# Swapping two DMA queues in the attention stage: key, query and value loads to SyncE, gates, branch weights and memory outputs to GpSimd

## The chip, the cores and the metric

One Trainium2 chip, of which the program uses one core. The metric is the device time of one execution in microseconds (us). The profile is one execution of the same program, taken by the hardware profiler. SP is the engine that does nothing here but issue DMAs; GpSimd (POOL) issues DMAs too, but also runs elementwise work.

## What is computed

A decoder block over 1024 positions of width 1024: half a feed-forward step, a mixer, half a feed-forward step. The mixer is what matters here:

```
y_a = dsa_attention(...) @ w_dsa_o      # 8 heads, width 64, causal, top-256 keys
y_b = conv_module(...) @ w_conv_out
y_m = memory_attention(...) @ w_mem_o   # 4 heads, into 256 memory tokens
g_a, g_b, g_m = split(sigmoid(gate_logits), 3)
merged = g_a * y_a + g_b * y_b + g_m * y_m
return x + rms_norm(merged @ w_out, mix_post_g)
```

Everything is float32. A product is done as three matmuls on a high and a low part of each operand.

## The kernel before

Earlier stages write what attention needs to DRAM: `qk_spill` (`self.qk`, 8 x 2 x 128 x 1024: four rows of queries, four of keys, each two heads wide, with the high part and the low part as an axis of two), `v_spill`, `gate_spill` (`self.sig`, three gates of 8 blocks of 128 x 1024) and `branch_spill` (`self.br`, the memory attention's outputs). On chip, tiles are taken from 50 slots of 4 KB per partition, alone or in small rings, and a load into a tile can start only when the last reader of that slot is done.

`attn` walks over two halves of the positions (c = 0, 1) and over 8 heads in each. For a head it loads a K tile and a Q tile from the ring `qk` (4 slots, so two heads at a time): `load_stack` (L794) fetches K, and the first half of Q, with the view `self.qk[row, :, e*64:e*64+64, lo:hi]`, whose outermost axis is that axis of two; L822 fetches the second half of Q in two pieces of 64 rows. K is 256 KB in the first half of the stage and 512 KB in the second; Q is 256 KB and twice 128 KB. `load_v` (L787) fetches the value tiles, 512 KB each, for four heads at a time. L851 is the score product, L855 to L861 the softmax, L893 the transposes, L881 the product with V.

`mix` interleaves with this the generator `outputs`, the branch stream: `branch` for the convolution, then for the memory attention (its inputs `om` come at L1110), then for the first half of the attention. Each takes four weight tiles of 512 KB (`weight`, L134), and for each of 8 blocks a gate (`sigr`, L925, ring `st` of two slots), multiplies a product in PSUM by the gate on VectorE (L936) and adds it to the partial sum on GpSimd (L943, in the last branch L938). After `attn` comes the second half of the attention's branch, then the output projection, with weights `woutr`.

A scheduler fixes each engine's order when the kernel is built. TensorE runs its list in that order: if the scores of a head wait for their K or Q, the branch stream's matmuls behind them wait too.

The source of the K load is this:

```
self.nc.gpsimd.dma_start(dst.bitcast(F32), self.qk[row, :, e * 64:e * 64 + 64, lo:hi])
```

Of the kernel before, what the change touches and what calls it, by code (L numbers as in the profile page):

```python
# [8 lines left out]
F32 = mybir.dt.float32  # L9
# [9 lines left out]
P = 128  # L19
# [25 lines left out]
class Kern:  # L45
# [83 lines left out]
        self.nc.scalar.activation(hi, raw, AF.Copy)  # L129
        self.nc.vector.tensor_sub(lo, raw, hi.bitcast(F32))  # L130

    def weight(self, name, src, shape, ring="w", raw="wr"):
        raw = self.rt(raw, name + "r", shape)
        self.nc.sync.dma_start(raw, src)  # L134
        if ring:
            hi, lo = self.rt(ring, name + "h", shape, F32R), self.rt(ring, name + "l", shape, F32R)
        else:
            hi, lo = self.blk(name + "h", shape, F32R), self.blk(name + "l", shape, F32R)
        self.split(hi, lo, raw)
        return hi, lo  # L140
# [640 lines left out]
    def load_v(self, grp, c):  # L781

        nc = self.nc
        V = []
        for t2 in range(2 * c + 2):
            v = self.blk("v", [P, 8, P], F32R)
            nc.gpsimd.dma_start(v.bitcast(F32).rearrange("p (t h) d -> p t (h d)", t=2),  # L787
                              self.vs[2 * t2:2 * t2 + 2, :, grp * 512:grp * 512 + 512].rearrange("t p c -> p t c"))
            V.append(v)
        return V  # L790

    def load_stack(self, dst, row, e, lo, hi):

        self.nc.gpsimd.dma_start(dst.bitcast(F32), self.qk[row, :, e * 64:e * 64 + 64, lo:hi])  # L794

    def behind(self, ins, *before):

# [5 lines left out]
    def attn(self):  # L803


        nc, S = self.nc, self.S
        O = S["O"]
        prev = V = None
        self.filled = None
        for c in range(2):  # L810
            if c:
                self.banks(s=[(0, 1)], tp=[2, 3, 4], po=[5], fl=[6, 7])
            for h in range(H_A):
                e = h % 2
                if e == 0:
                    O.append(self.blk("O", [P, 2, 512], F32R))
                K = self.rt("qk", "K", [P, (4 * c + 4) * P], F32R)
                Q = self.rt("qk", "Q", [P, 2, 512], F32R)
                self.load_stack(K, 4 + h // 2, e, 0, (4 * c + 4) * P)
                self.load_stack(Q[:, 0], h // 2, e, c * 512, c * 512 + 512)  # L820
                for r in range(2):
                    nc.gpsimd.dma_start(Q[r * 64:r * 64 + 64, 1].bitcast(F32),  # L822
                                      self.qk[h // 2, 1 - r, e * 64:e * 64 + 64, c * 512:c * 512 + 512])
                for g in range(2):
                    i0 = 4 * c + 2 * g
                    p, qk = self.weights_of(Q, K, i0)
                    yield (0.2 * i0 + 0.3) * FILL_A[i0 // 4]
                    if prev:
                        yield from self.weigh(*prev, qk)
                    if h % 4 == 0 and g == 0:  # L830
                        if V:
                            self.free(V)
                        V = self.load_v(h // 4, c)
                    prev = (h, g, i0, p, V, O[-1])
        yield from self.weigh(*prev, None)
        self.free(V)
# [78 lines left out]
    def branch(self, get, w, b, halves=(0, 1), last=None, group="fl"):  # L915

        nc, part = self.nc, self.S["part"]
        lo, nh = halves[0] * 512, len(halves) * 512
        first = not part
        for f2 in range(KT // 2):  # L920
            wt = self.weight("wo", w[:, f2 * 256:(f2 + 1) * 256].rearrange("(k p) f -> p k f", p=P), [P, 4, 256])
            for q in range(2):
                f = 2 * f2 + q
                s = self.rt("st", "sigr", [P, nh])
                nc.sync.dma_start(s, self.sig[b, f, :, lo:lo + nh])  # L925
                if first:
                    part.append(self.blk("part", [P, T]))
                for c in halves:
                    py = self.bank(group)
                    cs = slice(c * 512 - lo, c * 512 - lo + 512)  # L930
                    pr = part[f][:, c * 512:c * 512 + 512]
                    for k in range(4):
                        self.filled = self.mm3(py, (wt[0][:, k, q * P:(q + 1) * P], wt[1][:, k, q * P:(q + 1) * P]), get(k, c), k == 0, k == 3)
                        if k == 1:
                            yield 1.3
                    nc.vector.tensor_mul(pr if first else s[:, cs], py, s[:, cs])  # L936
                    if last:
                        nc.gpsimd.tensor_add(s[:, cs], s[:, cs], pr)  # L938
                        mb = self.blk("mg", [P, 2, 512], F32R)
                        self.split(mb[:, 0], mb[:, 1], s[:, cs])  # L940
                        last[c].append(mb)
                    elif not first:
                        nc.gpsimd.tensor_add(pr, s[:, cs], pr)  # L943
                    if c != halves[-1]:
                        yield 1.3
                yield 1.3
# [26 lines left out]
    def build(self):  # L973
        nc, A, S = self.nc, self.A, self.S
# [128 lines left out]
        def outputs():  # L1103
            half = lambda B: lambda k, c: tuple(x[:, c * 512:c * 512 + 512] for x in B[k])
            yield from self.branch(half(cb), A["w_conv_out"], 1)
            self.free(*cb)
            om = [tuple(self.blk("om", [P, T], F32R) for _ in range(2)) for _ in range(4)]
            for h in range(4):
                for r in range(2):
                    nc.sync.dma_start(om[h][r].bitcast(F32), self.br[h, r])  # L1110
            yield from self.branch(half(om), A["w_mem_o"], 2)
            self.free(*om)
            yield from y_a(0, "fl")
            self.free(O[:4])

        fill = outputs()
        self.mix(self.attn(), fill, 1.0)
        for _ in fill:
# [9 lines left out]
        wo = [self.weight("wout", A["w_out"][k * P:(k + 1) * P], [P, D], None) for k in range(KT)]  # L1128
# [7 lines left out]
        for t in range(NT):  # L1136
            c, s = t // 4, slice((t % 4) * P, (t % 4 + 1) * P)
# [348 lines left out]
```

## Time and profile before

| | us |
|---|---|
| time, median of 3 runs (2323.55 to 2325.48) | 2324.51 |
| the profiled execution's own time | 2322.4 |
| its span | 2320.6 |
| TensorE busy in the span | 2229.6 (96%) |
| VectorE busy | 1713.9 (74%) |
| ScalarE busy | 1168.0 (50%) |
| GpSimd busy | 380.9 (16%) |

The attention stage with its branch stream lies at about 1262 to 1524 us of the span, and the second half of the attention's branch at 1524 to 1575. In the page's 40 slices the TensorE digit falls below 9 only at the start, in the 23rd to 25th slice (58 us each, together 1276 to 1450), in the 29th and in the last. The page's DMA section splits the traffic into q1 (hardware, issued by SP: 195.94 MB) and q0 (software, issued by GpSimd: 21.09 MB).

### The profile page before, as it was taken

To read this page: it belongs to the slowest core of one execution; us is meant where nothing else is said; L and a number is where in the kernel's file an instruction comes from. 1 tells how busy PE (TensorE), PEld (TensorE's weight loads), DVE (VectorE), ACT (ScalarE), POOL (GpSimd) and SP (SyncE) were. 2 spreads that over 40 slices of the span, in tenths; PEclk is the share of its full clock that TensorE was granted. 3 is DMA by queue.
4 is the path that set the end of the run, shared out by engine and by line. 5 is a ranking of instruction groups with operands and counts; after the bars stand their busy time and mean duration, and the time that the engine had idled before them with its cause. 6 is when DMAs were issued, how large, how long until landed. Compare 5 with 4: busy or idle time off the path is not lost. (4 is left out here: it accounts for less than half of the span.)

```text
span 2320.6 us, 29086 instructions
## 1 busy us (share of the span) xinstructions
PE 2229.6 (96%) x10800; PEld 1374.5 (59%) x10800; DVE 1713.9 (74%) x3000; ACT 1168.0 (50%) x1971; POOL 380.9 (16%) x338
## 2 busy tenths in 40 slices
PE   8799999999999999999999788999899999999998
PEld 6344444444447987888887677878644444444443
DVE  7887777766577699997558677885877777777657
ACT  6644444444435343598996454453564444444423
POOL 2221111111100000120001213330321111111200
PEclk9799999999999999999999899999999999999999
DMA  8121111111224105334322655443421111111112
GB/s 290 37 64 55 55 60 59 55 55 55 86 70 156 51 28 204 127 123 131 102 96 95 179 153 157 140 155 122 140 78 63 57 60 58 55 55 55 45 56 91
DMA packets 162291, 218.87 MB, mean 94 GB/s; under 512 B 26052, under 2 KB 122820, under 8 KB 162150
## 3 DMA queue, kind: packets, MB, share of 16 engines
q1 hardware_dynamic: 137894, 195.94, 25.8%
q0 software_dynamic: 24256, 21.09, 3.5%
q8 instruction: 84, 1.38, 0.2%
q14 instruction: 57, 0.47, 0.1%
HBM read 171.79 MB, written 45.09 MB: 93 GB/s over the span
## 5 line engine op out<-in xcount | busy, mean ns | idle before, releaser
L146 PE MATMUL banks<-wds,h 128*128 128x512 f16 x704 | 266.8, 379 | 2.5 <-DVE h L262 2.5
L144 PE MATMUL banks<-xh,wts 128*128 128x512 f16 x704 | 267.5, 380 | 0.9 <-ACT xh L282 0.8
L145 PE MATMUL banks<-xl,wts 128*128 128x512 f16 x704 | 267.0, 379 | 0.0
L146 PE MATMUL banks<-xh,wts 128*128 128x512 f16 x704 | 267.0, 379 | 0.0
L145 PE MATMUL banks<-wds,h 128*128 128x512 f16 x704 | 266.8, 379 | 0.0
L144 PE MATMUL banks<-wds,h 128*128 128x512 f16 x704 | 266.7, 379 | 0.0
L1363 DVE SCALAR_TENSOR_TENSOR y<-banks,scal,y 128x512 f32<-128x512 f32 x288 | 209.5, 748 | 76.0 <-PE banks L146 65.6
L144 PE MATMUL banks<-xh,wh 128*128 128x512 f32 x576 | 226.2, 393 | 0.0
L146 PE MATMUL banks<-xh,wl 128*128 128x512 f32 x576 | 226.0, 393 | 0.0
L145 PE MATMUL banks<-xl,wh 128*128 128x512 f32 x576 | 225.4, 391 | 0.0
L144 PE MATMUL banks<-xh,wt 128*128 128x512 f16 x528 | 202.1, 383 | 4.3 <-DVE t L214 2.7
L146 PE MATMUL banks<-xh,wt 128*128 128x512 f16 x528 | 201.6, 382 | 0.8 <-DVE wt L262 0.8
L145 PE MATMUL banks<-xl,wt 128*128 128x512 f16 x528 | 201.6, 382 | 0.0
L261 ACT ACTIVATE wds<-wd,scal 128x1024 f16<-128x1024 f32 x44 | 47.9, 1139 | 252.0 <-DVE scal L230 229.4
L611 DVE SCALAR_TENSOR_TENSOR acc<-u,convc,acc 128x1023 f32<-128x1023 f32 (+14 forms) x120 | 151.7, 1264 | 0.9
L1311 ACT ACTIVATE sil<-sil,scal 128x512 f32<-128x512 f32 x88 | 63.2, 718 | 141.8 <-DVE sil L1310 141.8
L471 ACT ACTIVATE junka<-sc,tk_neg,tk_sg 128x512 bf16<-128x512 f32 (+1 forms) x124 | 124.1, 1001 | 12.4 <-DVE tk_cand L489 9.4
L1216 POOL TENSOR_TENSOR ws<-wg 128x512 f32<-128x512 f32 x22 | 44.8, 2035 | 501.9 <-DVE wds L262 381.1
L245 ACT ACTIVATE junka<-sil 128x1024 bf16<-128x1024 f32 x44 | 46.5, 1057 | 150.9 <-DVE sil L1327 150.9
L146 PEld LDWEIGHTS banks<-xh,wl 128*128 128x128 f32 x576 | 108.4, 188 | 22.4 <-DVE wl L130 0.2
L145 PEld LDWEIGHTS banks<-xl,wh 128*128 128x128 f32 x576 | 108.5, 188 | 21.6
L144 PEld LDWEIGHTS banks<-xh,wh 128*128 128x128 f32 x576 | 108.3, 188 | 21.2 <-ACT xh L129 0.3
(367 smaller groups left out, 4852.6 us busy)
## 6 DMA issues: line engine op xcount, KB each, us to landing
wg<-in_ffn_w_gu SPq DMA_DIRECT2D x44, 512.0 KB, 3.7
wu<-in_ffn_w_gu SPq DMA_DIRECT2D x44, 512.0 KB, 3.6
wd<-in_ffn_w_down SPq DMA_DIRECT2D x44, 512.0 KB, 4.3
wr<-in_w_in SPq DMA_DIRECT2D x38, 512.0 KB, 3.6
gate_spill<-st SPq DMA_DIRECT2D x24, 512.0 KB, 2.8
x_spill<-xres SPq DMA_DIRECT2D x16, 512.0 KB, 2.6
qk_spill<-qst SPq DMA_DIRECT2D x32, 256.0 KB, 2.7
sigr<-gate_spill SPq DMA_DIRECT2D x16, 512.0 KB, 5.0
```

Of the source, the lines that this page charges most:

```text
L144: self.first = mm(out, a[0], b[0], start=start, stop=False)
L145: mm(out, a[0], b[1], start=False, stop=False)
L146: return mm(out, a[1], b[0], start=False, stop=stop)
L245: self.nc.scalar.activation(self.junk(x.shape), x, AF.Square, accum_out=ss)
L261: self.nc.scalar.activation(hi, raw, AF.Copy, scale=s)
L471: nc.scalar.activation(self.junk((P, ns[q])), sc[q], AF.Sign, bias=bias[:, z:z + 1], scale=scale, accum_out=cnt[:, z:z + 1])
L611: nc.vector.scalar_tensor_tensor(a[:, s:], u[:, :T - s], self.cc[:, m, j:j + 1], a[:, s:], op0=OP.mult, op1=OP.add)
L1216: V.tensor_add(a[:, 0], lo[:, :, P:], hi[:, :, P:])
L1311: nc.scalar.activation(o, o, AF.Silu, scale=iv)
L1363: V.scalar_tensor_tensor(self.y[t][:, cs], py, iv, self.y[t][:, cs], op0=OP.mult, op1=OP.add)
```

## The change

Three issue sites, of K, Q and V, go from GpSimd's queue to SP's; the branch stream's weights, gates and memory outputs go from SP's to GpSimd's. `weight` gets an argument for the queue.

```
-    def weight(self, name, src, shape, ring="w", raw="wr"):
+    def weight(self, name, src, shape, ring="w", raw="wr", q=None):
         raw = self.rt(raw, name + "r", shape)
-        self.nc.sync.dma_start(raw, src)
+        (q or self.nc.sync).dma_start(raw, src)
...
-            nc.gpsimd.dma_start(v.bitcast(F32).rearrange("p (t h) d -> p t (h d)", t=2),
+            nc.sync.dma_start(v.bitcast(F32).rearrange("p (t h) d -> p t (h d)", t=2),
...
-        self.nc.gpsimd.dma_start(dst.bitcast(F32), self.qk[row, :, e * 64:e * 64 + 64, lo:hi])
+        self.nc.sync.dma_start(dst.bitcast(F32), self.qk[row, :, e * 64:e * 64 + 64, lo:hi])
...
-                    nc.gpsimd.dma_start(Q[r * 64:r * 64 + 64, 1].bitcast(F32),
+                    nc.sync.dma_start(Q[r * 64:r * 64 + 64, 1].bitcast(F32),
...
-            wt = self.weight("wo", w[:, f2 * 256:(f2 + 1) * 256].rearrange("(k p) f -> p k f", p=P), [P, 4, 256])
+            wt = self.weight("wo", w[:, f2 * 256:(f2 + 1) * 256].rearrange("(k p) f -> p k f", p=P), [P, 4, 256], q=nc.gpsimd)
...
-                nc.sync.dma_start(s, self.sig[b, f, :, lo:lo + nh])
+                nc.gpsimd.dma_start(s, self.sig[b, f, :, lo:lo + nh])
...
-                    nc.sync.dma_start(om[h][r].bitcast(F32), self.br[h, r])
+                    nc.gpsimd.dma_start(om[h][r].bitcast(F32), self.br[h, r])
```

On SP, in the middle of the second half of attention (c = 1), the list before is the branch stream's own; `wor` are branch weights, `sigr` gates:

```order
L134 DMA wor<-in_w_mem_o 128x4x256
L925 DMA sigr<-gate_spill 128x1024 x2
L134 DMA wor<-in_w_dsa_o 128x4x256
L925 DMA sigr<-gate_spill 128x1024 x2
L134 DMA wor<-in_w_dsa_o 128x4x256
```

In the changed kernel the same engine has there:

```order
L794 DMA K<-qk_spill 128x1x1024
L794 DMA Q<-qk_spill 128x1x512
L822 DMA Q<-qk_spill 64x512 x2
L787 DMA v<-v_spill 128x2x512
L794 DMA K<-qk_spill 128x1x1024
L794 DMA Q<-qk_spill 128x1x512
L822 DMA Q<-qk_spill 64x512 x2
L794 DMA K<-qk_spill 128x1x1024
```

From the start of attention to its end nothing but K, Q and V stands on SP, apart from two last gate stores; the output projection's `woutr` loads follow directly behind the last head's.

On GpSimd, at the start of the memory branch's additions (L943), the list before is:

```order
L794 DMA K<-qk_spill 128x1x1024
L794 DMA Q<-qk_spill 128x1x512
L822 DMA Q<-qk_spill 64x512 x2
L943 TENSOR_TENSOR part<-sigr,part 128x512 x3
L794 DMA K<-qk_spill 128x1x1024
L794 DMA Q<-qk_spill 128x1x512
L822 DMA Q<-qk_spill 64x512 x2
L943 TENSOR_TENSOR part<-sigr,part 128x512 x3
```

And in the changed kernel:

```order
L925 DMA sigr<-gate_spill 128x1024
L134 DMA wor<-in_w_mem_o 128x4x256
L943 TENSOR_TENSOR part<-sigr,part 128x512 x2
L925 DMA sigr<-gate_spill 128x1024
L943 TENSOR_TENSOR part<-sigr,part 128x512 x2
L925 DMA sigr<-gate_spill 128x1024
L134 DMA wor<-in_w_dsa_o 128x4x256
L943 TENSOR_TENSOR part<-sigr,part 128x512 x2
```

The additions no longer stand behind K loads, but each pair of them stands between the gate loads whose slots it frees.

In the last branch, where GpSimd's additions (L938) feed the merged tiles, the changed kernel has on GpSimd:

```order
L134 DMA wor<-in_w_dsa_o 128x4x256
L938 TENSOR_TENSOR sigr<-sigr,part 128x512
L134 DMA wor<-in_w_dsa_o 128x4x256
L925 DMA sigr<-gate_spill 128x512
L134 DMA wor<-in_w_dsa_o 128x4x256
L938 TENSOR_TENSOR sigr<-sigr,part 128x512
L134 DMA wor<-in_w_dsa_o 128x4x256
```

Before, the sixteen L938 stand there in one row, with no DMA between them. TensorE's list changes in a few places only, where neighbouring matmuls swap.

## Rows read from the trace of the kernel before

**Rows 1.** Engines by stage (busy us, instructions); then granted clock, DMA share, GB/s.

```profile
core 0: us, PE busy (x) PEld busy (x) DVE busy (x) ACT busy (x) POOL busy (x), PEclk, DMA share, GB/s
1050.00:1100.00 50.00, 50.00 (x223) 41.39 (x222) 35.01 (x81) 43.41 (x78) 2.73 (x4) 1.00 0.42 126
...
1279.00:1361.00 82.00, 63.38 (x344) 51.57 (x342) 56.76 (x170) 39.48 (x99) 22.48 (x33) 0.92 0.65 172
1361.00:1524.00 163.00, 148.67 (x829) 125.92 (x830) 124.43 (x225) 77.09 (x140) 47.19 (x48) 0.96 0.47 139
1524.00:1575.00 51.00, 49.18 (x235) 40.00 (x234) 42.93 (x53) 25.92 (x37) 19.92 (x13) 1.00 0.65 217
```

**Rows 2.** What TensorE waited for, 1240 to 1660: total, times, longest.

```profile
PE banks L851 <- DMA Q<-qk_spill: 21.7, 8, 9.1
PE banks L145 <- DMA om<-branch_spill: 4.8, 2, 3.7
```

**Rows 3.** DMA issues, 1240 to 1600: queue, count, KB each, median us to landing.

```profile
sigr<-gate_spill SPq DMA_DIRECT2D x16, 512.0 KB, 5.0
v<-v_spill POOLq DMA_DIRECT2D x12, 512.0 KB, 8.6
om<-branch_spill SPq DMA_DIRECT2D x8, 512.0 KB, 5.8
K<-qk_spill POOLq DMA_DIRECT2D x8, 512.0 KB, 16.9
wor<-in_w_dsa_o SPq DMA_DIRECT2D x8, 512.0 KB, 4.5
sigr<-gate_spill SPq DMA_DIRECT2D x16, 256.0 KB, 2.9
Q<-qk_spill POOLq DMA_DIRECT2D x14, 256.0 KB, 15.5
```

**Rows 4.** DMA queue q0 (GpSimd's): packets, MB, share; in 1494:1498, then 1436:1440.

```profile
q0 software_dynamic: 75, 0.17, 11.2%
...
q0 software_dynamic: 36, 0.13, 8.2%
```

**Rows 5.** SP's issues of the convolution's constants (first start us), then short stretches, as rows 1.

```profile
L594 SPq DMA_DIRECT2D taps<-in_w_dw x1: 304/304/304, 717.3 to 717.3; - x1
L596 SPq DMA_DIRECT2D taps<-in_conv_ln_b x1: 251/251/251, 718.2 to 718.2; - x1
722.60:722.80 0.20, 0.20 (x2) 0.19 (x1) 0.20 (x2) 0.20 (x1) 0.00 (x0) 1.00 0.07 26
722.80:723.00 0.20, 0.20 (x2) 0.16 (x1) 0.20 (x1) 0.20 (x1) 0.00 (x0) 1.00 0.07 21
1282.00:1286.00 4.00, 4.00 (x26) 3.17 (x25) 2.67 (x10) 1.87 (x7) 0.42 (x1) 1.00 1.10 374
```

**Rows 6.** TensorE in order of time: start, us, tiles [idle before it, and what ended it].

```profile
1298.02 0.45 PE L851 MATMUL banks<-K,Q 128*128 128x128 f32 x1 [9.09 <-DMA Q<-qk_spill]
1364.87 1.69 PE L851 MATMUL banks<-K,Q 128*128 128x320 f32 x4 [5.53 <-DMA Q<-qk_spill]
1508.72 0.75 PE L851 MATMUL banks<-K,Q 128*128 128x320 f32 x4
```

**Rows 7.** GpSimd in order of time, columns as rows 6: the stage's first K load.

```profile
1278.92 0.85 POOL L794 DMA_DIRECT2D K<-qk_spill  x1 [3.12 <-PE banks L851]
```

**Rows 8.** DMA issues in 1266:1269, columns as rows 3.

```profile
v<-v_spill POOLq DMA_DIRECT2D x1, 512.0 KB, 4.7
```

**Rows 9.** What SP's queue waited for, 1240 to 1600: its longest total.

```profile
SPq L925 <- POOL part L943: 97.1, 8, 20.0
```

**Rows 10.** GpSimd's last additions: count, min/median/max ns, first and last start.

```profile
L938 POOL TENSOR_TENSOR sigr<-sigr,part x16: 1274/1294/2204, 1507.2 to 1571.5; 128x512 f32<-128x512 f32 x16
```

**Rows 11.** Stretches of low granted clock, columns as rows 1.

```profile
1292.70:1302.90 10.20, 3.50 (x13) 3.09 (x14) 1.59 (x8) 1.09 (x4) 0.53 (x1) 0.50 0.64 157
...
1364.40:1371.20 6.80, 6.33 (x23) 5.67 (x24) 2.44 (x7) 1.94 (x5) 0.00 (x0) 0.50 0.21 66
```

## The prediction

> **What bounds the kernel now.** I read the stretches first. TensorE is the bound of the whole, and in the attention stage it loses time: 18.6 us idle of 82 in the first part, 14.3 of 163 in the second, 1.8 of 51 behind it [rows 1]. The list of TensorE's waits says where: 21.7 us in eight waits of the scores for Q, loaded on GpSimd's queue, and 4.8 us for the memory outputs [rows 2]. The largest single ones are 9.09 us at 1298 and 5.53 us at 1365 [rows 6]. So the stage is held, now and then, by K and Q landing late. The issue list shows the contrast on which the change plays: K of 512 KB takes 16.9 us from GpSimd's queue, Q of 256 KB 15.5 us, while `om`, gates and weights of 512 KB take 4.5 to 5.8 us from SP's [rows 3]. The question is whether that is the queue or the shape of the load.
>
> **Why K and Q are slow.** V answers half of it: same queue, same 512 KB, but 8.6 us [rows 3], and 4.7 us for one early in the stage [rows 8]. What differs is the view: K and the first half of Q are read through an outermost axis of two, V and `om` through 128 partitions. Late in a head's load, when little else moves, GpSimd's queue had 11.2% of 16 engines' time, which is 1.8 engines, and moved 0.17 MB in those 7.2 engine-us: 23.7 GB/s on each [rows 4]. The other stretch gives 24.8 GB/s. So such a load is confined to about two engines, and the queue has data for them all the time; 374 GB/s is what all sixteen do [rows 5].
>
> Does SP's queue confine too? The convolution's constants are the only narrow loads that SP issues: 31 rows of 2 KB and three single rows, all issued between 717.3 and 718.2. At 722.6 to 723.0 data still moves, at 0.07 of sixteen engines, one engine, and 21 to 26 GB/s [rows 5]. Four loads issued within 1 us, 70 kB in all, and one engine's worth still moving 4 us later: SP's queue confines a narrow load as well, and puts different narrow loads on the same engine. I therefore take it that K and the first half of Q, issued by SP, all go through one pair of engines, head after head.
>
> [...]
>
> **The change, part by part.**
>
> *K, Q, V to SP.* Issuing costs less (0.25 to 0.38 us on SP against 0.85 us on GpSimd [rows 5, 7]), which is off the path. The load itself: on each engine of the pair, a head of the first half needs (262 + 262)/2 kB for K and Q's first half and 262/16 for the two 64-row pieces, 278 kB; a head of the second half (524 + 262)/2 + 16 = 410 kB. Two heads are loaded before the stage; behind the first K load at 1278.9 [rows 7] come six heads of the first kind and eight of the second: 4950 kB. The same two engines carry a sixteenth of all else: 7 V tiles, 14 gates of 512 KB, 6 of 256 KB, 8 weights and 8 `om`, 40 times 512 KB in all (of the loads in rows 3 and the memory branch's four weights, those issued between 1281 and the last head's scores), at 32.8 kB each 1310 kB. Together 6260 kB, at 24.8 GB/s 252 us. The first bytes move some 2 us after the issue (a 256 KB gate takes 2.9 us to land, of which 0.7 is data at 374 GB/s), so the last head's K and Q land at about 1281 + 252 = 1533. Its scores now start at 1508.7 [rows 6]. **+25 us**, if the pair never idles. It hardly can: a head's load is issued when the scores of the head two before are done, and by then the pair is still busy with the head between. At 23.7 GB/s it is 264 us and +36; without the gates', weights' and `om`s' share 209 us, which ends before 1508.7, so the lower end is 0. I take 25, since the share comes through the same engines in any order, and 24.8 is the stretch with the fewest other packets.
>
> The waits of today are not to be subtracted: they are inside 1508.7, and the new ones take their place. TensorE idles ahead of nearly every head from the fourth on, and its static order lets no branch work fill that.
>
> *Branch stream to GpSimd.* 56 loads leave SP. Landing on GpSimd's queue costs 4.7 us at best and 8.6 at the median for 512 KB, against 4.5 to 5.8 now [rows 3, 8]. A gate has two slots and about a block's 10 us until it is used, so 3 us more stays covered. What covers it goes when landing passes some 12 us. The additions L943 come out from behind K loads. SP waited 97.1 us for them [rows 9], but TensorE shows no wait for that, so I cost it at nothing: what is late next is Q anyway.
>
> *The last branch (1524 to 1575).* GpSimd now has an addition of 1.29 us, a gate load (some 0.75 us of issue) and half a weight load per block, about 2.4 us, under the 4.3 us at which the sixteen additions come on average (1507.2 to 1571.5 [rows 10]). TensorE is 49.2 of 51 us busy there [rows 1], so there is little cover: a gate that lands 1 us later through three slots is up to 3 us over eight blocks, a weight load stuck behind a wait some 2 more. Ends 0 and +5; I take **+2**.
>
> *Before the stage.* The first two heads' loads go to SP among the gate stage's weights, at 1047 to 1068. Engine time 4 times 5.3 us on the pair; TensorE never idles there (50.00 of 50 us [rows 1]) and two pairs of weight tiles let a weight come a block ahead: 0. If that cover were gone, up to 5.
>
> *Sum.* 25 + 2 = 27 us on the profiled execution's 2322.4, 2349.4; the median is 2.1 above it: **2351**. The forecast's own range, with the tail's ends, is 2336 (half of the stream's share hidden: 12 us) to 2366 (36 + 5).
>
> **Rivals.**
>
> *1. SP spreads these loads over all engines.* Then K and Q land in about 5 us like `om`, the 21.7 us go, and with them half of TensorE's busy time in the low-clock stretches behind the waits, (3.5 + 6.3)/2, 5 us [rows 11]: about 2298. For it speak the 4.5 to 5.8 us of every wide load on SP; against it the constants' one engine. [...]
>
> *2. Narrow, but not all on one pair.* If K and Q's first half fall on different pairs, the busier engine has 6 x 147 + 8 x 278 + 1310 = 4420 kB, 178 us: not a bound. Landing falls to about 8 and 13 us, the 5.53 us wait and the ones of 1 to 2 us go, the 9.09 us one, behind the V burst, stays: about 2313.
>
> *3. The pair's backlog is just covered.* K, Q and V alone take 209 us of the 228 between 1281 and 1508.7. If the branch stream's packets take no more than the gaps that this leaves, the scores wait about as long as now: 2324, no change. Against it: 40 transfers at 1.3 us are 53 us, and the gaps are 19.
>
> *4. GpSimd's queue becomes a bound too.* The gates land in 15 us instead of 5 (as K does now), two slots turn in 15 + 8 us, 11.5 per block against 10: 1.5 us on 14 blocks, on top of the forecast: 2372.
>
> **How the numbers follow.** Forecast 0.60, rivals in order 0.12, 0.11, 0.08, 0.09. A measurement here can tell about 0.2%, 4.6 us. Faster is rivals 1 and 2: 0.23. Same is rival 3: 0.08. Slower is the forecast and rival 4: 0.69. The range leaves out rival 1 and the upper half of rival 4: 2308 to 2370.
>
> **What the changed profile would show.** If right: K and Q landings on SP of 12 us in the first half, and 20 to 40 in the second, growing from head to head; TensorE's wait for K and Q of 40 us or more, spread over most heads; the last head's scores near 1533; DMA share low while TensorE waits; L943 without long waits. If K lands in 5 us, or the waits for Q vanish, the step from the constants to K is wrong. If waits for gates or weights lead TensorE's list, the branch stream's cover is.

## The result, and the profile after

The changed kernel takes 2376.32 us (median of 6 runs, 2373.49 to 2378.89) beside 2322.98 for the kernel before in the same session: ratio 1.0228, 95% interval 1.0217 to 1.0239. It is slower by 53 us. The forecast was 2351, with a range that ended at 2370: the sign and the place were right, the size was half of what came.

The profiled execution's span grew from 2320.6 to 2371.7 us, by 51.1. The engines by stage, to be read beside [rows 1]:

```profile
core 0: us, PE busy (x) PEld busy (x) DVE busy (x) ACT busy (x) POOL busy (x), PEclk, DMA share, GB/s
1050.00:1100.00 50.00, 50.00 (x222) 41.43 (x221) 34.93 (x83) 44.88 (x80) 0.00 (x0) 1.00 0.37 117
1279.00:1361.00 82.00, 56.24 (x270) 46.62 (x269) 44.18 (x133) 29.83 (x74) 4.22 (x7) 0.83 0.39 130
1361.00:1524.00 163.00, 129.00 (x669) 107.67 (x667) 99.13 (x193) 61.67 (x118) 31.11 (x35) 0.86 0.40 131
1524.00:1600.00 76.00, 71.59 (x388) 59.90 (x389) 62.33 (x102) 41.73 (x69) 31.50 (x32) 1.00 0.36 126
1600.00:1630.00 30.00, 25.55 (x96) 19.79 (x95) 21.63 (x27) 10.64 (x14) 10.50 (x8) 0.83 0.54 181
```

Ahead of the stage TensorE loses nothing. In it TensorE is idle for 25.8 us of the first 82 (18.6 before) and 34.0 of the next 163 (14.3 before), while the DMA share falls from 0.65 to 0.39 and from 0.47 to 0.40. More idle and less DMA at once fits a few busy DMA engines among idle ones; the stretches below show two. TensorE's granted clock is lower as well, 0.83 and 0.86 instead of 0.92 and 0.96, so part of the loss is work at a lower clock and not idle time. What TensorE waited for, 1240 to 1720 (total us, times, longest), beside [rows 2]:

```profile
PE banks L851 <- DMA Q<-qk_spill: 42.3, 15, 8.7
PE banks L881 <- DMA v<-v_spill: 7.8, 1, 7.8
...
PE banks L145 <- DVE woutl L130: 4.1, 2, 3.4
PE banks L257 <- DVE scal L254: 3.7, 1, 3.7
PE banks L145 <- DMA om<-branch_spill: 3.5, 2, 2.8
```

The wait for Q doubled, from 21.7 to 42.3; the other new ones are one for V and one for `woutl`, a weight of the output projection. The stream's gates cause no wait of TensorE, and its loads land as follows (queue, count, KB each, median us to landing), beside [rows 3]:

```profile
sigr<-gate_spill POOLq DMA_DIRECT2D x16, 512.0 KB, 7.1
...
om<-branch_spill POOLq DMA_DIRECT2D x8, 512.0 KB, 9.3
...
wor<-in_w_dsa_o POOLq DMA_DIRECT2D x8, 512.0 KB, 4.9
...
Q<-qk_spill SPq DMA_DIRECT2D x28, 128.0 KB, 15.2
```

For K and for the first half of Q the profile gives no landing on SP's queue; the 64-row pieces of Q behind them take 15.2 us. How busy the DMA engines are with K alone shows in SP's queue, q1, at 1387 to 1395 (packets, MB, share of sixteen engines), to be read beside [rows 4]:

```profile
DMA packets 106, 0.44 MB, mean 55 GB/s; under 512 B 1, under 2 KB 1, under 8 KB 105
...
q1 hardware_dynamic: 105, 0.42, 12.9%
```

And at 1465 to 1467, with a burst of GpSimd's queue, q0, beside it:

```profile
q0 software_dynamic: 124, 0.45, 91.3%
q1 hardware_dynamic: 16, 0.07, 12.9%
```

12.9% of sixteen is 2.06 engines: two, and busy all the time. In the quiet stretch they move 0.42 MB in 8 x 2.06 = 16.5 engine-us, 25.5 GB/s on each. Beside the burst it is sixteen packets of 4 KB in 4.1 engine-us, 16 GB/s. And at 1436 to 1441, behind a burst:

```profile
q0 software_dynamic: 42, 0.13, 6.8%
q1 hardware_dynamic: 32, 0.13, 6.6%
```

Together that is 13.4%, two engines again: what is left of the stream's burst goes, as it seems, by the same pair as K.

The chain of work that ended last, 1370 to 1560 (by line, then pieces with start and us), says the same from the other side. Its head is SP standing at an issue:

```profile
by line: SPq L822 19.9%; DMA Q<-qk_spill 9.1%; PE banks L881 8.4%; DMA v<-v_spill 7.0%; PE banks L851 6.7%; DMA om<-branch_spill 6.4%; PE banks L146 6.1%; PE banks L144 5.9%; PE banks L145 5.7%; PE banks L893 4.9%; SPq L794 3.5%; issue 2.9%
...
1382.70 11.96 SPq L822
1394.71 17.30 DMA Q<-qk_spill
...
1425.21 12.11 DMA om<-branch_spill
...
1477.71 13.16 SPq L822
1491.61 13.38 DMA v<-v_spill
```

Where the 51.1 us arise, by the first score product of some heads (us of the span, counted from 0; eight heads in each half) and by two marks behind them:

| | before | after | difference |
|---|---|---|---|
| head 2 | 1298.0 | 1295.9 | -2.1 |
| head 8 (first of the second half) | 1364.9 | 1387.2 | +22.3 |
| head 9 | 1382.9 | 1410.6 | +27.7 |
| head 12 | 1448.6 | 1480.5 | +31.9 |
| head 13 | 1469.1 | 1510.9 | +41.8 |
| head 15 | 1508.7 | 1550.6 | +41.9 |
| last addition L938 starts | 1571.5 | 1616.5 | +45.0 |
| end of the span | 2320.6 | 2371.7 | +51.1 |

### The profile page after: what moved, and what is told of

It is laid out like the page before. It is cut to its first block, busy times and chain, and to the rows that moved or that the text cites. A ratio compares the mean times of both kernels' runs of the same rounds, so it can differ in the third digit from the quotient of the medians.

```text
span 2371.7 us, 29050 instructions
## 1 busy us (share of the span) xinstructions
PE 2247.0 (95%) x10800; PEld 1386.9 (58%) x10800; DVE 1716.2 (72%) x3000; ACT 1168.5 (49%) x1971; POOL 365.0 (15%) x318
## 4 chain that ended last, share of the span: by engine, by line
PE 67%; DVE 12%; ACT 7%; DMA 5%; issue 4%; SPq 3%; POOL 1%; ACTq 0%; DVEq 0%; POOLq 0%
PE banks L146 21%; PE banks L144 21%; PE banks L145 21%; ACT junka L471 4%; SPq L822 2%; DMA Q<-qk_spill 2%; DVE acc L611 2%; PE banks L881 1%; PE banks L851 1%; SPq L794 1%; PE banks L893 1%; DVE wts L262 1%; ACT junka L170 1%; DMA v<-v_spill 1%; DVE xl L283 1%
## 5 line engine op out<-in xcount | busy, mean ns | idle before, releaser
L146 PEld LDWEIGHTS banks<-xh,wl 128*128 128x128 f32 x576 | 108.4, 188 | 22.3 <-DVE wl L130 0.2
```

Source lines behind the costliest of these rows:

```text
L146: return mm(out, a[1], b[0], start=False, stop=stop)
```

## Experiments

Each is timed against the kernel before; "head 15 at" gives the start of that head's first score product.

**Shape or queue.** The first pair makes K and the first half of Q wide, in the changed kernel and in the kernel before: two loads of 64 rows in place of one whose outermost axis is two.

```
-        self.nc.sync.dma_start(dst.bitcast(F32), self.qk[row, :, e * 64:e * 64 + 64, lo:hi])
+        for r in range(2):
+            self.nc.sync.dma_start(dst[r * 64:r * 64 + 64].bitcast(F32), self.qk[row, r, e * 64:e * 64 + 64, lo:hi])
```

> The changed kernel with K and the first half of Q each read in two pieces of 64 rows, as the second half of Q already is; queues as changed. Theory (the view with an outermost axis of two confines these loads to one pair of DMA engines on SP's queue): K lands in 4 to 7 us, the 42 us of TensorE's waits for Q, the 8 us one for V and SP's long issues (up to 14 us) go, and with them the 22 us of such waits that the kernel before has; the 9 us lost behind the last head stay. 2324.5 - 22 + 9 = 2311, 2295 to 2316. Rival (the queue or the branch stream on GpSimd is the cause, not the shape): the waits stay, 2360 to 2378. Rival (pair and queue half each): about 2340.

> The kernel before with the same 64-row pieces for K and the first half of Q, all queues as before. Theory (shape): K lands in 6 to 9 us instead of 16.9, most of the 21.7 us of waits for Q go, some of it comes back in GpSimd's longer issues (one more issue of 0.85 us for each of two loads): 2300 to 2312. Rival (the queue is what makes K and Q slow): K still 15 us or more, 2318 to 2328.

Measured: the changed kernel with wide loads 2295.96 us, ratio 0.9879 (0.9865 to 0.9894); the kernel before with wide loads, on GpSimd's queue (`gpsimd` in place of `sync` in the lines above), 2292.31, ratio 0.9859 (0.9844 to 0.9873). TensorE's wait for Q falls to 1.1 us in the first and 0.5 us in the second. K's two pieces land in 4.3 us on SP's queue, by the issue list of the first:

```profile
K<-qk_spill SPq DMA_DIRECT2D x16, 256.0 KB, 4.3
```

and in 4.2 us on GpSimd's, by that of the second:

```profile
K<-qk_spill POOLq DMA_DIRECT2D x16, 256.0 KB, 4.2
```

The second came 8 us below its expected range. That range counted the waits for Q alone; with wide loads the waits for `om` fall as well, from 5.2 us to 0.6, and the granted clock is 1.00 in both stretches of the stage. How the 8 us divide was not worked out.

So it is the shape. It makes the 42 us, and it made the 22 us of waiting that the kernel before already had. With wide loads the queue hardly matters in the stage: head 15 comes at 1478.8 and at 1477.6.

**Which half of the change.** One run moves only K, Q and V to SP, the other moves only the stream to GpSimd. For the second, the three attention loads read as before:

```
-        self.nc.sync.dma_start(dst.bitcast(F32), self.qk[row, :, e * 64:e * 64 + 64, lo:hi])
+        self.nc.gpsimd.dma_start(dst.bitcast(F32), self.qk[row, :, e * 64:e * 64 + 64, lo:hi])
...
```

> Half of the change: K, Q and V go to SP's queue, the branch stream stays there too. Theory (the pair is the bound whichever queue the stream is on): last head's scores at 1545 to 1560, and gates and weights now stand behind SP's long issues, so no better than the whole change: 2360 to 2395. Rival (the stream on GpSimd is the cause): 2320 to 2330.

> The other half: branch stream to GpSimd's queue, K, Q and V stay there. Theory (the pair on SP's queue is the cause of the 42 us up to the last head): last head's scores within 10 us of before (1509), what remains is the 9 us behind the last head: 2322 to 2340. Rival (the stream on GpSimd is the cause): 2355 to 2380.

Measured: K, Q and V alone 2372.0 us, 1.0200 (1.0183 to 1.0217), head 15 at 1558.4. The stream alone 2319.32, 0.9979 (0.9968 to 0.9989), head 15 at 1497.6, 11 us earlier than before. The loss sits in K, Q and V. The stream's half gains 11 us up to head 15 and gives back 8 behind it (the tail, below); the expectation, 2322 to 2340, was too high by 3. In its trace the waits for Q are 14.4 us instead of 21.7, and those for `om` 0.6 instead of 5.2; what makes them shorter was not tested. The shapes of K and Q are the same narrow ones in all of these kernels; on GpSimd's queue they cost 21.7 us of waits before and 14.4 with the stream moved, on SP's 42.3 in either case.

**How much on the pair.** K alone wide, then the first half of Q alone wide (the loop above, for `row >= 4` or `row < 4` only), and the three loads of Q in their old shapes on GpSimd's queue with K narrow on SP's.

> The changed kernel with K alone in two pieces of 64 rows; the first half of Q stays narrow. Theory (bytes on the pair): the pair then carries 131 kB for a head's Q plus sixteenths, some 180 kB a head in the second half instead of 410, 7 us of 20: not a bound, 2296 to 2306, near both wide (2296). Rival (any narrow load on SP holds the list behind it, whatever its size): waits of some 3 us a head stay, 2320 to 2345.

> The changed kernel with the first half of Q alone in two pieces of 64 rows; K stays narrow. Theory (bytes on the pair): 164 kB a head in the first half, 295 in the second, 6 x 164 + 6 x 295 + 1250 of the stream = 4000 kB up to head 13, 161 us, done by 1442 while head 13 now starts at 1469: no backlog, but each K still takes over 10 us, so waits about as before or less: 2305 to 2325. Rival (any narrow load on SP, or the narrow K whatever else is on the pair): 2340 to 2378.

> The changed kernel with all three loads of Q on GpSimd's queue, in their old shapes; K and V stay on SP's. All bytes of a head stay as narrow as they were, but K's and Q's go by two queues. Theory (on SP's queue every narrow load takes the same pair, on GpSimd's another): SP's pair carries K alone, as in the run with Q wide (2329, last head's scores at 1508), and Q goes past it; GpSimd's list gets three more issues a head: 2320 to 2345. Rival (both queues use the same pair, or narrow bytes cost the same wherever they go): 2360 to 2378.

| narrow loads on SP | ratio (95%) | median us | head 2 to head 8, a head | head 8 to head 13, a head | head 15 |
|---|---|---|---|---|---|
| none (both wide) | 0.9879 (0.9865 to 0.9894) | 2295.96 | 9.1 | 18.8 | 1478.8 |
| Q's first half | 0.9966 (0.9954 to 0.9978) | 2316.88 | 10.7 | 19.2 | 1492.9 |
| K | 1.0016 (1.0007 to 1.0026) | 2329.41 | 11.5 | 20.8 | 1508.0 |
| K, with narrow Q on GpSimd | 1.0043 (1.0029 to 1.0057) | 2335.14 | 12.0 | 20.9 | 1514.5 |
| both (the change) | 1.0228 (1.0217 to 1.0239) | 2376.32 | 15.2 | 24.7 | 1550.6 |

The two middle columns are differences of first score products, divided by six and by five heads. More narrow bytes on SP's queue, later heads, and more than in proportion: 14 us for Q alone, 29 for K alone, 72 for both. Two of three expectations missed on the low side, by 11 and 4 us. They set the pair against the second half alone. The first half is an estimate here: TensorE needs only 9 us a head there, and a narrow load of 131 kB on each of two engines takes 131 / 24.8 = 5.3 us at the rate of [rows 4], to which the stream's burst there adds its share, so that even one narrow load can hold heads back. The third run has every narrow byte of the change, yet is 41 us faster than it, and within 6 of the run where Q is wide: so Q's narrow loads on GpSimd's queue go, for the most part, past the engines that K's take on SP's. Its trace has stretches that show it. At 1476 to 1478:

```profile
q0 software_dynamic: 44, 0.08, 13.2%
q1 hardware_dynamic: 22, 0.09, 12.6%
```

That is two engines for each queue, four in all. That K's and Q's narrow loads share one pair on SP's queue is what costs: 41 us between this run and the change (2335.14 and 2376.32).

Which two engines a queue takes for a load, and by what choice, no trace here shows. On SP's queue two loads of 64 rows in place of each load with an outermost axis of two gain 80 us (2376.32 to 2295.96).

**What else stood on SP's list.** V back on GpSimd's queue; and Q's 64-row pieces issued ahead of K, so that they don't wait behind a narrow load:

> The changed kernel with V back on GpSimd's queue; K and Q stay on SP's, the branch stream on GpSimd's. In the changed kernel TensorE waited 7.8 us for one V tile (for head 12, issued on SP behind K and Q), and the heads behind it follow at the pace of TensorE, so its delay stays to the end. Theory (V's own wait is a part of the 42 us, on top of the pair): the wait for V goes, heads 13 to 15 come 4 to 8 us earlier, 2368 to 2373. Rival (the pair is the whole of it, the next K or Q takes V's place): 2374 to 2379.

> The changed kernel with the two 64-row pieces of Q issued ahead of K and of the first half of Q. In the changed kernel SP stands up to 14 us at an issue while the pair of DMA engines has its queue full, and these pieces stand behind the narrow loads, so they are issued only when K is nearly through. Theory (the pair's bytes are the bound; the late pieces cost only the 1 to 3 us by which they land behind the narrow ones, and no byte goes away): 2366 to 2378. Rival (SP's blocked issues are what makes the heads late): 2340 to 2362.

Measured: V back 2371.91 us, 1.0206 (1.0190 to 1.0222), head 15 at 1550.5; pieces first 2376.55, 1.0222 (1.0199 to 1.0244), head 15 at 1552.8. With V back its wait of 7.8 us is gone, and the next wait for Q is there (start, us, tiles, idle before):

```profile
1501.90 0.65 PE L881 MATMUL banks<-pT,v 128*128 128x256 f32 x4 [1.02 <-DMA v<-v_spill]
...
1509.43 1.79 PE L851 MATMUL banks<-K,Q 128*128 128x320 f32 x4 [4.54 <-DMA Q<-qk_spill]
```

So V only stood in the same line. The time fell into the theory's range, but not by its road: head 13 came at 1509.4 instead of 1510.9 and head 15 where it was, so what this kernel may have gained (the intervals overlap) lies behind head 15. The rival's mechanism holds, the next Q takes V's place. The pieces put first are issued without the long stand (count: min/median/max ns, first and last start), and nothing is won. The changed kernel:

```profile
L822 SPq DMA_DIRECT2D Q<-qk_spill x28: 588/3916/14242, 1278.3 to 1535.4; - x28
```

With the pieces first:

```profile
L820 SPq DMA_DIRECT2D Q<-qk_spill x28: 482/596/2377, 1278.9 to 1528.2; - x28
...
L794 SPq DMA_DIRECT2D Q<-qk_spill x14: 520/2496/10902, 1280.8 to 1529.4; - x14
```

So the long stand at the pieces goes with the narrow loads ahead of them and is not a cost of its own. SP still stands at the first half of Q in this run (L794), for up to 10.9 us and 2.5 in the median; a list without any such stand was run only with wide loads, so a cost of those other stands is not excluded. Five kernels with K and Q narrow on SP (the change, K, Q and V alone, V back, pieces first, and the next one) have head 15 between 1550.5 and 1558.4, whatever else is done with the lists.

**The tail.** The last branch's weights and gates back on SP:

```
-            wt = self.weight("wo", w[:, f2 * 256:(f2 + 1) * 256].rearrange("(k p) f -> p k f", p=P), [P, 4, 256], q=nc.gpsimd)
+            wt = self.weight("wo", w[:, f2 * 256:(f2 + 1) * 256].rearrange("(k p) f -> p k f", p=P), [P, 4, 256], q=None if group == "one" else nc.gpsimd)
...
-                nc.gpsimd.dma_start(s, self.sig[b, f, :, lo:lo + nh])
+                (nc.sync if group == "one" else nc.gpsimd).dma_start(s, self.sig[b, f, :, lo:lo + nh])
```

> The changed kernel with the gates and weights of the last branch (second half of the attention's output) back on SP's queue. It lost 9.4 us behind the last head's scores: 3 up to the last addition, where VectorE waits for gates, 6 behind it, where the weights' low parts stand behind the scaling of a gain vector on VectorE. Theory (both come from this branch's loads on GpSimd's queue, which let SP run ahead and change the order behind): 2365 to 2370. Rival (they come from the late stage itself, the clock or the order of the heads): 2373 to 2379.

Measured: 2368.61 us, 1.0191 (1.0172 to 1.0211), span 2365.5, 6.2 less than the change. From head 15 to the end this kernel takes 814.5 us, the change 821.1, the kernel before 811.9: 6.6 of the 9.2 us are this branch's loads on GpSimd's queue. The other 2.6 stay open; the run with K, Q and V alone on SP loses nothing there (811.8 us), which points to the stream's move for them too. In the changed kernel VectorE meets there (start, us, tiles, idle before):

```profile
1603.59 0.69 DVE L936 TENSOR_TENSOR sigr<-banks,sigr 128x512 f32<-128x512 f32 x1 [0.75 <-DMA sigr<-gate_spill]
...
1608.64 0.69 DVE L936 TENSOR_TENSOR sigr<-banks,sigr 128x512 f32<-128x512 f32 x1 [0.94 <-DMA sigr<-gate_spill]
...
1610.38 2.32 DVE L237 CUSTOM_DVE_ANT_0 junkv<-gpre 128x1024 bf16<-128x1024 f32 x1
...
1614.20 1.61 DVE L239 TENSOR_SCALAR gpre<-gpre,scal 128x1024 f32<-128x1024 f32 x1
...
1616.33 1.21 DVE L130 TENSOR_TENSOR woutl<-woutr,wouth 128x1024 fp32r<-128x1024 f32 x1
...
1619.97 2.35 DVE L130 TENSOR_TENSOR woutl<-woutr,wouth 128x1024 fp32r<-128x1024 f32 x2
```

Two gates come late. And with the branch's loads off SP's list, the load of `gpre`, a gain vector, moved ahead of the last `woutr`, so its scaling (L237 to L239) now stands ahead of the last low parts of the weights. TensorE waits for those, and then runs at 0.63 us a product instead of 0.39:

```profile
1612.99 0.39 PE L146 MATMUL banks<-wouth,mg 128*128 128x512 f32 x1
...
1617.59 0.79 PE L145 MATMUL banks<-woutl,mg 128*128 128x512 f32 x1 [3.39 <-DVE woutl L130]
1618.18 0.63 PE L146 MATMUL banks<-wouth,mg 128*128 128x512 f32 x1
...
1621.25 0.80 PE L145 MATMUL banks<-woutl,mg 128*128 128x512 f32 x1 [0.73 <-DVE woutl L130]
...
1626.32 0.39 PE L145 MATMUL banks<-woutl,mg 128*128 128x512 f32 x1
```

The granted clock of that stretch is 0.50; in steps of 1 us it is 1.00 up to 1615, 0.50 from 1616 to 1626 and 1.00 again from 1627:

```profile
1617.00:1626.00 9.00, 7.68 (x17) 5.65 (x18) 5.24 (x6) 1.58 (x2) 1.67 (x1) 0.50 0.25 98
```

The low clock lies around the waits of 3.39 and 0.73 us; products start every 0.43 us there instead of 0.23, so the seventeen of them cost 3.4 us more. Before, the same place had one wait of 0.57, and a granted clock of 1.00 (1574 to 1582). With the tail back `gpre` is loaded behind the last `woutr` again, and TensorE's one wait there is this:

```profile
1618.19 0.50 PE L145 MATMUL banks<-woutl,mg 128*128 128x512 f32 x1 [0.56 <-DVE woutl L130]
```

**What beats both.** Wide loads with the last branch on SP, and wide loads with everything of the stage on SP:

> K and Q in 64-row pieces on SP's queue, the branch stream on GpSimd's, but the last branch's gates and weights on SP's: the run with both wide (2296) and the one with the tail back (6 us better than the change) together. Theory (they are two separate costs): 2286 to 2292, as fast as the kernel before with wide loads (2292) or a little faster. Rival (with K and Q on time the tail's cost is hidden or comes another way): 2294 to 2298.

> K and Q in 64-row pieces, and everything of the attention stage on SP's queue, the branch stream too. Theory (with wide loads the queue makes no difference in the stage, and the tail is as before): 2286 to 2294. Rival (the split over two queues is worth something once the shapes are wide: loads that wait for a slot hold others on one list): 2297 to 2310.

Measured: 2290.6 us, 0.9852 (0.9830 to 0.9873), and 2287.52 us, 0.9839 (0.9818 to 0.9861). With the kernel before in wide loads (0.9859) these are three versions some 1.5% faster than the kernel before; the intervals don't tell them apart. The simplest is all on one queue. Its two stretches, beside [rows 1]:

```profile
1279.00:1361.00 82.00, 80.40 (x462) 66.46 (x461) 72.42 (x207) 50.46 (x121) 0.00 (x0) 1.00 0.73 222
1361.00:1524.00 163.00, 157.09 (x882) 133.01 (x882) 135.81 (x230) 84.77 (x149) 39.85 (x28) 1.00 0.49 149
```

TensorE is idle 1.6 us of the first 82, and the granted clock is 1.00 in both.

## Why the prediction was right, and where it was not

*The mechanism held.* K and the first half of Q are narrow on SP's queue too, as the step from [rows 4] and the constants of [rows 5] had it, and all go through one pair. The trace after shows 2.06 busy engines, the two runs with wide loads lose the waits, and the run with Q on GpSimd's queue is 41 us faster. Rivals 1 and 2 fall with these, and rival 3 with the result. Rival 4 asked for gates that land in 15 us: they landed in 7.1, and TensorE's waits in the stage show no gate.

*The step that failed is the size of the term for K, Q and V: 25 us in the sum, 41.9 measured.* Its sum said that the pair is done at 1533. It was done at 1545. SP's queue in 1542 to 1545:

```profile
q1 hardware_dynamic: 62, 0.12, 11.2%
```

and in 1545 to 1548:

```profile
q1 hardware_dynamic: 6, 0.01, 0.7%
```

264 us instead of 252 for the 6260 kB: 23.7 GB/s on average, which the working had as its upper end, +36, and not 24.8, which it took because that stretch was the quietest. This choice was the wrong way round. The backlog ran through the bursts too, and in the burst shown above each engine of the pair gave SP's queue 16 GB/s. Gaps between loads play little part: of the half-microsecond steps from 1281 to 1545, only twelve, 6 us in all, have a DMA share of 0.11 or less, which is under 1.9 engines. The count of bytes was a little high, which makes the exact 23.7 partly luck. From 1281 to 1545 the two queues moved:

```profile
q1 hardware_dynamic: 7777, 16.77, 18.9%
q0 software_dynamic: 4381, 15.90, 18.5%
```

SP's 16.77 MB are as counted, but GpSimd's are 15.90 MB and not the 17.3 of the 33 loads in the count. That leaves 6170 kB on each engine of the pair, 23.4 GB/s; an even sixteenth of every wide load on each engine is the author's estimate in both sums.

The other 6 us are a head that the step did not look at. It took the last head as the one that the pair holds. In fact the delay was complete at head 13 (+41.8), held by V and, with V elsewhere, by Q; from there to head 15 TensorE needs 39.7 us, as before (39.6), so the delay that is there at head 13 is not made good, and the scores come 5.6 us after the last bytes. The sum has two slips, neither of which moves its main line. Half of the stream's share (33 loads of 32.8 kB at 24.8 GB/s, 44 us) is 22 us and would leave +3 at head 15, not the 12 of the range's lower end. And rival 3 counts 53 us for 40 transfers where the 7 of V are in its 209 us already; it is the same 44 us against 19 of gaps. The step on V, costed as a sixteenth of bytes alone, also left out that V stands behind K and Q on SP's list: in the chain above the load of V comes behind a stand of 13.2 us and then takes 13.4 itself.

*The second term that failed is the last branch: +2, with +5 as the end; it measured 9.2.* A gate that lands late was foreseen and is there, 3 us up to the last addition. Not foreseen were the 6 behind it: what leaves SP's list lets the loads behind it change places, VectorE's order follows, and a wait of 3.4 us follows, with the granted clock at 0.50 around it. The pace that this step used was also too slow: of the sixteen additions L938 the first eight belong to the first half of the attention's branch, where L938 stands too, and the last branch's own eight come every 3.3 us (1548.2 to 1571.5 before), not 4.3; GpSimd's 2.4 us a block still fit. The move of `gpre` could have been read from the order of the changed kernel, a few rows behind the place that was read.

*Costed at nothing, and so it was:* the stretch before the stage (50.00 of 50 us) and the additions behind K loads. The issues, also at nothing, were not cheaper as the step had them: the pieces held SP for 3.9 us in the median, where they had taken 0.56 on GpSimd; with the stand at the pieces taken away nothing was won. The stream's move in the stage, also costed at nothing, is worth some 11 us when K and Q stay on GpSimd (head 15 at 1497.6 against 1508.7); in the change the pair hides it.

*The sum.* 41.9 + 9.2 = 51.1 us against 27, and against 41 with both terms at their upper ends. *What the changed profile would show* came as written for the wait for Q (42.3, in fifteen waits), the DMA share and the additions; the last head's scores, near 1533 in the forecast, came at 1550.6. The landings, forecast at 20 to 40 us in the second half, can't be read for K; the pieces of Q behind it took 10.7 to 25.9 us over the whole stage, beside 8.8 to 19.1 before.

## What to carry to other kernels

When a load takes twice as long as another of the same size on the same queue (here 16.9 us beside 8.6), look at its outermost axis before moving it: splitting this one into two loads of 64 rows was worth 30 us or more on either queue, while moving it cost 53. If a few DMA engines are the bound, cost them at the average rate with the bursts of other traffic in (here 23.4 GB/s on each), not at the quiet rate (24.8), and make the sum at each consumer, not only at the last. And when loads are moved off a list, read what closes up behind them to the end of the next stage.

## What the runs showed of the hardware that was not expected

An issue on SP was not always short: in the changed kernel one DMA instruction held SP for up to 14.2 us (median 3.9 for the 64-row pieces), while with wide loads and everything on SP the same pieces held it for at most 0.61 us. In one such stand of 12.0 us, from 1382.7, the DMA share was 0.13, two engines of sixteen; what SP stands for there no view shows. On GpSimd's queue the same pieces took 0.53 to 0.97 us to issue in the kernel before. And the same narrow loads on the two queues are far apart in what they cost: 14.4 us of waits with all of them on GpSimd's and the stream beside them, 42.3 with all on SP's.
